# Splitting the second block's weights on POOL during the last feed-forward stage

## The chip, the cores and the metric

The kernel runs on one core of a Trainium2 chip. The time is device microseconds of one execution, taken as the median of 3 runs. TensorE (PE in the rows) multiplies, VectorE (DVE), ScalarE (ACT) and GpSimd (POOL) work on tiles in SBUF, and SyncE (SP) issues most of the DMAs.

## The reference, cut to what matters

The program is a model of two parts on 512 tokens of 1024 channels, batch 1, in float32. The first part has two layers, each with a mixer, cross attention and a gated feed-forward stage with a convolution over three tokens; the second part is one block that mixes a recurrence over chunks of 64 tokens with banded attention:

```
first_block, for layer in 0, 1:
    x = layer_norm(alpha * x + mixer(x))
    x = layer_norm(alpha * x + cross_attend(x, mem))
    x = layer_norm(alpha * x + conv_ffn(x))        # up: 1024 -> 2 x 2816, down: 2816 -> 1024
second_block:
    h = rms_norm(x, norm_g) * (1 + scale) + shift
    proj = h @ w_in                                # 1024 -> 2176 (r, k, v, g, decays) + 2048 (q, k, v, g)
    y_r = rwkv7_mix(token_shift(proj[:, :2176]))   # 8 heads of 64, a state per head
    y_a = chunk_band_attention(proj[:, 2176:])     # 8 heads of 64, 9 chunks of 64 keys
    x = x + gate * (concat(y_r * silu(g_r), y_a * silu(g_a)) @ w_out)
```

Weights are inputs, so each is read from HBM once per execution (two of the `w_in` slices twice).

## The kernel before

Activations lie with channels on the 128 partitions, 8 tiles of 128x512. A matmul in float32 is done as three products in float32r (`mm3`, lines 261 to 265): each operand is kept as a high part, rounded to float32r, and a low part, the remainder. So a weight piece of 128x1024 is loaded as it is into a `raw` tile (`piece`, line 239; SP issues the DMA), ScalarE casts it into the high half of a tile of the weight ring (line 229) and another engine subtracts to get the low half (line 230). In the first part that engine is VectorE; in the second block, where `self.extra` is 0, it is POOL. The ring has four `w` tiles, and two more (`wx`) while the first part runs; there are two `raw` tiles and a third (`rawx`) in the first part.

`lin` (line 267) does a product with stationary weights: for each block of 128 output channels, 24 matmuls (8 channel tiles, three products) into a PSUM bank, and then a function `epi` on the result. `ffn` (line 619) is the feed-forward stage. It goes through the 22 tiles of 128 inner channels in three chunks of 8, 8 and 6. For each inner tile there are two blocks upward; the gate's result goes through the convolution and a gelu, the other is multiplied with it and split into an `hd` tile (22 of these upward steps a layer). After each chunk 8 blocks go downward and are added to the residual `x` (lines 648 and 650). At the end of the last chunk POOL sums `x` and its squares over the channel tiles (`res_stat`, lines 370 and 371) for the layer norm (`ln_half`), and takes part in the norm itself (line 400).

`open2` (line 723) starts the second block while the last norm is going on: it computes the blocks `OPEN = (16, 0, 4, 8, 1)` of `w_in`. `block2` then has one line of work with long waits: four head pairs (`rwkv_pair`, line 866), the inversion of each chunk's triangular matrix (`rwkv_invert`, line 991, 31 steps of lines 1003 and 1005 on VectorE), and the chain of states (`rwkv_chain`). All else, the other blocks of `w_in`, attention and the start of `w_out`, stands as generators in `ORDER` (line 48): `r` and `q` are blocks of `w_in`, `v` the attention's values, `g` gates, `p` and `a` attention, `y` gated results and `o` the output. `fill` (line 775) puts some microseconds of it wherever the line of work waits; each entry may start only at its milestone (the number beside it). `lin_g` (line 839) is such a block; it gets its weights through `piece` too, as do `att_v` (line 1129), `out_begin` and `out_end`.

No queue's order is written out by hand as a whole. A planner orders each engine's instructions by the program's order and by when it expects their inputs and tiles to be ready, so an engine's queue is not always in the order of the code. A tile's next user waits until all users of its former content are done.

Of the kernel before, what the change touches and what calls it, by code (L numbers as in the profile page):

```python
# [172 lines left out]
class Prog:  # L173
# [69 lines left out]

    def raw(self):
        self.n += 1
        if self.extra and self.n0 % 3 == 2:
            self.n0 += 1
            return self.t("rawx", [P, 1024], F32, 1)
        self.n0 += 1
        return self.keep.tile([P, 1024], F32, tag="raw", name=f"raw_{self.n}", bufs=2)  # L250

    def wtile(self):
        """The weights' ring: some of its room is there only in the first block."""
        self.nw += 1
        if self.extra and self.nw % (4 + self.extra) >= 4:
            return self.t("wx", [P, 2, 1024], F32R, self.extra)
        self.n += 1
        return self.keep.tile([P, 2, 1024], F32R, tag="w", name=f"w_{self.n}", bufs=4)
# [8 lines left out]
    def lin(self, src, ms, xs, epi, n=S, first=0, last=0):  # L267
        """The first (last) few blocks go through one half of the tokens, then through the other, for the LN
        before (after) them; epi(m, psum, tokens) gets the last ones by halves."""
# [43 lines left out]
    def flush(self):  # L313
        """The LN that is due."""
        while self.pending:
            ts = self.pending.pop(0)
            self.ln_half(ts)
            if self.norm[0] == "ln_ffn_g" and self.norm[2] == 1:
                self.modulate(ts)

    def lin_tm(self, src, pieces, xs, ntok, epi):
        """out[tok tiles][128, 512 cols]: activations stationary, weights moving."""
        banks = [self.bank() for _ in range(ntok)]
        for j, pc in enumerate(pieces):
            w = self.piece(self.a[src][pc])
            for kk in range(2):
                k = 2 * j + kk
                cs = slice(kk * 512, kk * 512 + 512)
                for s in range(ntok):
                    ss = slice(s * P, s * P + P)  # L330
                    self.mm3(banks[s], (xs[k][0][:, ss], xs[k][1][:, ss]), (w[:, 0, cs], w[:, 1, cs]),
                             k == 0, k == 7)
        for s in range(ntok):
            epi(s, banks[s])
# [8 lines left out]
    def rsqrt(self, y, t, v, eps):  # L343
        """y = (v + eps) ** -0.5: the table's value and a Newton step; eps is a column of self.eps."""
# [7 lines left out]
    # residual, then LN over the channels  # L352
# [61 lines left out]
    # mixer of layer 0  # L414
# [204 lines left out]
    def ffn(self, l, xs):  # L619
        nc = self.nc  # L620
        for c, (f0, f1) in enumerate(CHUNKS):
# [3 lines left out]
            def epi(m, ps, ts):  # L625
# [9 lines left out]
                else:  # L635
                    h = self.tmp()
                    nc.vector.tensor_tensor(out=h, in0=ps, in1=keep["g"], op=ALU.mult)
                    hs.append(self.split(self.hd(), h))

# [5 lines left out]
            def epi_d(m, ps, ts):  # L645
# [5 lines left out]
                if c == 1 and l == 0 and m == 1:  # L651
                    self.ada_end()
                if c == 2:
                    self.res_stat(m, ts)
# [5 lines left out]
    # the modulation of the second block, gathered a piece at a time  # L660
# [23 lines left out]
    def ada_end(self):  # L684
        nc = self.nc
        # the sum over the partitions: within 32 of them by turning 32-blocks, then over the four groups
# [18 lines left out]
    def modulate(self, ts):  # L705
        """rms_norm(x) * norm_g * (1 + scale) + shift of half of the tokens."""
# [16 lines left out]
    def open2(self):  # L723
        """The second block's first products, of the first half of the tokens."""
# [48 lines left out]
    # The second block has one line of work with long waits (the states) and much other work for the tensor  # L773
    # engine: `bg` holds the latter as generators, and fill() puts some of it wherever the former waits.
# [57 lines left out]
    def mm(self, out, **kw):  # L832
        """A product on the line with the waits: it stays behind what fill() put before it."""
        self.tc.keep_in_program_order(self.nc.tensor.matmul(out, **kw))  # L834
# [4 lines left out]
    def lin_g(self, src, m, xs, epi, ks=range(KT)):  # L839
        w = self.piece(self.a[src][m])  # L840
# [25 lines left out]
    def rwkv_pair(self, j):  # L866
        """What the chunks of heads 2j and 2j+1 need."""
# [9 lines left out]
        # kk  # L877
# [12 lines left out]
        # k'  # L890
        nc.scalar.activation(u, av, AF.Identity, bias=self.ka1[:, j : j + 1], scale=self.v("k_a_2", j))
        nc.vector.tensor_tensor(out=k, in0=k, in1=u, op=ALU.mult)
        # bonus
# [7 lines left out]
        # decays  # L901
# [20 lines left out]
        # values by token  # L922
# [20 lines left out]
        # scores within the chunks  # L943
# [25 lines left out]
        # keys by token  # L969
# [10 lines left out]
        # the part of the right sides that no state enters  # L980
# [10 lines left out]
    def rwkv_invert(self, prs):  # L991
        """(I - N)^-1 of each chunk's strictly triangular N: 32-blocks by substitution, then the block between."""
# [58 lines left out]
    def rwkv_chain(self, prs, tt):  # L1051
# [40 lines left out]
        def line(i, pr):  # L1092
            for _ in chunks(i, pr):
                yield FILL[9]
            # group norm, then the gate
# [33 lines left out]
    def att_v(self, half, xs):  # L1129
        """Values of two token tiles."""  # L1130
        self.va += [self.t("va", [P, S], F32, 4) for _ in range(2)]
        banks = [self.bank() for _ in range(2)]
        for jj in range(4):
            w = self.piece(self.a["in_va"][jj])
# [12 lines left out]
    def att_epi(self, m, ps):  # L1147
        """Queries or keys of a pair of heads, normed."""
# [15 lines left out]
    def att_probs(self, j):  # L1164
        """Softmax of a pair of heads: a tile holds a chunk's queries of one head, then of the other."""
# [60 lines left out]
    def gate_epi(self, n):  # L1226
        """silu(x) = (tanh(x / 2) + 1) * x / 2; the half comes where it is used."""
# [22 lines left out]
    def out_begin(self):  # L1250
        """The residual, and the first products of w_out over what is there."""
# [5 lines left out]
        for m in range(NPART):  # L1257
            w, ps = self.piece(self.a["out"][m]), self.bank(("mm", "mm", "ch", "ch")[m])
# [9 lines left out]
    def out_end(self, out):  # L1268
        nc = self.nc
        rest = [k for k in range(KT) if k not in KS]  # L1270
        for m in range(8):
# [4 lines left out]
            else:  # L1276
                w, ps = self.piece(self.a["out"][m]), self.bank()
# [93 lines left out]
```

## Time and profile before

| | us |
|---|---|
| median of 3 runs | 1856.92 (1856.45 to 1857.71) |
| span of the profiled execution, first to last instruction | 1854.5 |
| PE busy | 1786.7 (96%) |
| VectorE busy | 1096.3 (59%) |
| ScalarE busy | 783.0 (42%) |
| POOL busy | 362.8 (20%) |

The median is 2.4 us above the span of the profiled execution. Stages in the trace: the last feed-forward stage runs from about 1046 to 1400 us, the norm and the opening to about 1437, pairs to about 1600, the inversion to 1661, the states to about 1800, the output to the end. A matmul's duration in a row is longer than the distance between two starts, since matmuls overlap. POOL's and VectorE's durations are from issue to end, so an instruction that stands still on its engine shows as a long one. A wait is put down to the releaser that came last.

### The profile page before, as it was taken

To read this page: it belongs to the slowest core of one execution; us is meant where nothing else is said; L and a number is where in the kernel's file an instruction comes from. 1 tells how busy PE (TensorE), PEld (TensorE's weight loads), DVE (VectorE), ACT (ScalarE), POOL (GpSimd) and SP (SyncE) were. 2 spreads that over 40 slices of the span, in tenths; PEclk is the share of its full clock that TensorE was granted. 3 is DMA by queue.
4 is the path that set the end of the run, shared out by engine and by line. 5 is a ranking of instruction groups with operands and counts; after the bars stand their busy time and mean duration, and the time that the engine had idled before them with its cause. 6 is when DMAs were issued, how large, how long until landed. Compare 5 with 4: busy or idle time off the path is not lost.

```text
span 1854.5 us, 26344 instructions
## 1 busy us (share of the span) xinstructions
PE 1786.7 (96%) x10476; PEld 1502.4 (81%) x10476; DVE 1096.3 (59%) x1741; ACT 783.0 (42%) x1319; POOL 362.8 (20%) x331
## 2 busy tenths in 40 slices
PE   8999998999999999999999999999998888879999
PEld 7889988888888888988998988888887766656657
DVE  5676689743463467444565764343447666975673
ACT  5444534532332356232453642232335645535561
POOL 0115014000000051000501400000015455623232
PEclk9999999999999999999999999999999999989999
DMA  8431455332322226333131242323222222222142
GB/s 279 145 103 60 132 181 188 100 102 91 102 92 91 80 64 196 112 96 100 59 104 35 69 125 92 102 92 100 88 86 73 82 75 88 89 74 81 56 160 103
DMA packets 62635, 192.25 MB, mean 104 GB/s; under 512 B 7344, under 2 KB 10032, under 8 KB 62512
## 3 DMA queue, kind: packets, MB, share of 16 engines
q1 hardware_dynamic: 54432, 172.25, 29.0%
q0 software_dynamic: 3248, 9.44, 1.5%
q10 hardware_dynamic: 4832, 8.88, 1.4%
q8 instruction: 82, 1.34, 0.3%
q14 instruction: 41, 0.34, 0.1%
HBM read 181.36 MB, written 9.18 MB: 103 GB/s over the span
## 4 chain that ended last, share of the span: by engine, by line
PE 76%; DVE 15%; ACT 3%; issue 3%; DMA 2%; POOL 0%; SPq 0%; DVEq 0%; ACTq 0%; POOLq 0%
PE ch L264 10%; PE ch L263 10%; PE ch L265 10%; PE mm L263 9%; PE mm L265 9%; PE mm L264 9%; PE pv L264 3%; PE pv L263 3%; PE pv L265 3%; PE ch L834 3%; DVE x L401 2%; DVE xh L405 1%; DVE w L230 1%; DVE x L400 1%; DVE vt L681 1%
## 5 line engine op out<-in xcount | busy, mean ns | idle before, releaser
L263 PE MATMUL mm<-xh,w 128*128 128x512 f32 (+1 forms) x704 | 266.1, 378 | 8.5 <-ACT w L229 7.5
L265 PE MATMUL mm<-xh,w 128*128 128x512 f32 (+1 forms) x704 | 258.6, 367 | 0.8 <-DVE w L230 0.8
L264 PE MATMUL mm<-xh,w 128*128 128x512 f32 (+1 forms) x704 | 259.0, 368 | 0.0
L370 POOL TENSOR_TENSOR t<-x,x 128x512 f32<-128x512 f32 x6 | 8.1, 1351 | 1011.1 <-ACT w L229 656.1
L229 ACT CAST w<-raw 128x1024 fp32r<-128x1024 f32 (+2 forms) x131 | 133.1, 1017 | 164.0 <-PE ch L265 62.9
L263 PEld LDWEIGHTS mm<-xh,w 128*128 128x128 f32 x704 | 135.6, 193 | 35.7 <-ACT w L229 7.8
L264 PE MATMUL ch<-xh,w 128*128 128x512 f32 (+1 forms) x432 | 154.1, 357 | 0.6 <-DVE xh L405 0.5
L264 PEld LDWEIGHTS mm<-xh,w 128*128 128x128 f32 x704 | 135.9, 193 | 22.9 <-issue 3.4
L263 PE MATMUL ch<-xh,w 128*128 128x512 f32 (+1 forms) x432 | 153.0, 354 | 1.3 <-ACT xh L404 1.3
L265 PE MATMUL ch<-xh,w 128*128 128x512 f32 (+1 forms) x432 | 152.7, 353 | 1.5 <-DVE w L230 1.5
L265 PEld LDWEIGHTS mm<-xh,w 128*128 128x128 f32 x704 | 135.8, 193 | 22.6 <-issue 1.1
L229 ACT CAST wx<-raw 128x1024 fp32r<-128x1024 f32 (+1 forms) x85 | 88.1, 1039 | 152.4 <-PE ch L265 71.5
L230 DVE TENSOR_TENSOR w<-rawx,w 128x1024 fp32r<-128x1024 f32 (+2 forms) x85 | 104.1, 1225 | 68.0 <-ACT w L229 67.6
L229 ACT CAST w<-rawx 128x1024 fp32r<-128x1024 f32 (+2 forms) x85 | 87.3, 1027 | 116.4 <-PE mm L265 71.0
L230 DVE TENSOR_TENSOR w<-raw,w 128x1024 fp32r<-128x1024 f32 (+2 forms) x90 | 113.0, 1257 | 37.8 <-ACT w L229 37.4
L230 DVE TENSOR_TENSOR wx<-raw,wx 128x1024 fp32r<-128x1024 f32 (+1 forms) x85 | 107.6, 1267 | 27.6 <-ACT wx L229 27.4
L230 POOL TENSOR_TENSOR w<-raw,w 128x1024 fp32r<-128x1024 f32 x41 | 100.4, 2456 | 119.0 <-ACT w L229 115.1
L263 PE MATMUL ch<-xh,wx 128*128 128x512 f32 (+1 forms) x304 | 103.5, 341 | 0.0
L265 PE MATMUL ch<-xh,wx 128*128 128x512 f32 (+1 forms) x304 | 103.0, 339 | 0.0
L264 PE MATMUL ch<-xh,wx 128*128 128x512 f32 (+1 forms) x304 | 103.0, 339 | 0.0
L263 PE MATMUL mm<-hd,w 128*128 128x256 f32 (+1 forms) x304 | 97.7, 322 | 3.6 <-ACT hd L229 3.6
L265 PE MATMUL mm<-hd,w 128*128 128x256 f32 (+1 forms) x304 | 97.9, 322 | 0.0
(484 smaller groups left out, 4498.6 us busy)
## 6 DMA issues: line engine op xcount, KB each, us to landing
raw<-in_up SPq DMA_DIRECT2D x56, 512.0 KB, 3.5
rawx<-in_up SPq DMA_DIRECT2D x32, 512.0 KB, 3.5
kt<-in_ada SPq DMA_DIRECT2D x48, 256.0 KB, 3.3
raw<-in_dn SPq DMA_DIRECT2D x24, 512.0 KB, 3.5
raw<-in_in_r SPq DMA_DIRECT2D x24, 512.0 KB, 3.5
raw<-in_c_in SPq DMA_DIRECT2D x16, 512.0 KB, 3.5
raw<-in_xo SPq DMA_DIRECT2D x12, 512.0 KB, 3.6
raw<-in_xv SPq DMA_DIRECT2D x11, 512.0 KB, 4.1
```

Of the source, the lines that this page charges most:

```text
L229: nc.scalar.copy(hi, src)
L230: (eng or nc.vector).tensor_tensor(out=lo, in0=src, in1=f32(hi), op=ALU.subtract)
L263: mm(out, lhsT=ah, rhs=bh, start=start, stop=False)
L264: mm(out, lhsT=ah, rhs=bl, start=False, stop=False)
L265: mm(out, lhsT=al, rhs=bh, start=False, stop=stop)
L370: eng.tensor_tensor(out=sz, in0=self.x[0][:, ts] if m == 1 else sz, in1=z, op=ALU.add)
L400: (nc.vector if k in DVE_SUB else nc.gpsimd).tensor_tensor(out=x, in0=x, in1=mn, op=ALU.subtract)
L401: nc.vector.scalar_tensor_tensor(out=x, in0=x, scalar=gk, in1=rs, op0=ALU.mult, op1=ALU.mult)
L405: nc.vector.scalar_tensor_tensor(out=lo, in0=x, scalar=bk, in1=f32(hi), op0=ALU.add, op1=ALU.subtract)
L681: nc.vector.scalar_tensor_tensor(out=dst, in0=raw, scalar=sc, in1=dst, op0=ALU.mult, op1=ALU.add)
L834: self.tc.keep_in_program_order(self.nc.tensor.matmul(out, **kw))
```

## The change

A preparation stage is added to the last feed-forward stage (`l == 1`). `pre_begin` lists the weight pieces of the second block in the order of their first use, without those of `OPEN`: 36 pieces, with the four of `in_va` once. `pre_step` is called after each of the 22 upward steps and after the 16 downward steps of the first two chunks. A call loads the next piece from POOL's queue into the lower half of a `vt` tile (two of 128x2x1024, which the attention before has left), after a copy of one column from the step's result into that place; that copy ties the load to the stage's progress. Then POOL does the split of the piece of the call before, copy and subtraction, and stores both halves, 1 MB, in HBM. In the second block `ready` takes the place of `piece` at all four callers: SP loads the finished 1 MB straight into a tile of the weight ring, with no cast on ScalarE and no subtraction on POOL there. The entry `(0, "r1")`, which computed block 1 once more though `OPEN` has it, leaves `ORDER`. The other lines of the diff take away comments.

```diff
@@ ORDER
-    (0, "r1"), (0, "r5"), (0, "r9"),
+    (0, "r5"), (0, "r9"),
@@ class Prog
+    def pre_begin(self):
+        self.prep, todo = {}, []
+        for _, ws in ORDER:
+            for w in ws.split("+"):
+                k, m = w[0], int(w[1:])
+                if k in "rq" and m not in OPEN:
+                    todo.append(("in_r", m))
+                elif k == "g":
+                    todo.append(("in_r", 12 + m) if m < 4 else ("in_ga", m - 4))
+                elif w == "v0":
+                    todo += [("in_va", i) for i in range(4)]
+                elif k == "o":
+                    todo += [("out", i) for i in range(8)]
+        self.todo, self.due2 = todo, []
+
+    def pre_step(self, at):
+        nc = self.nc
+        if self.todo:
+            key = self.todo.pop(0)
+            t = self.t("vt", [P, 2, D], F32, 2)
+            nc.gpsimd.tensor_copy(t[:, 1, 0:1], at[:, 0:1])
+            nc.gpsimd.dma_start(out=t[:, 1, :], in_=self.a[key[0]][key[1]])
+            self.due2.append((key, t))
+        if len(self.due2) > 1 or not self.todo:
+            for key, t in self.due2[:1]:
+                self.due2.pop(0)
+                hi, lo = t[:, 0, :].bitcast(F32R), t[:, 1, :].bitcast(F32R)
+                nc.gpsimd.tensor_copy(hi, t[:, 1, :])
+                nc.gpsimd.tensor_tensor(out=lo, in0=t[:, 1, :], in1=t[:, 0, :], op=ALU.subtract)
+                name = f"sp_{key[0]}{key[1]}"
+                d = self.prep[key] = self.dram.tile([P, 2, D], F32, tag=name, name=name)
+                nc.gpsimd.dma_start(out=d, in_=t)
+
+    def ready(self, src, m):
+        w = self.wtile()
+        self.nc.sync.dma_start(out=f32(w), in_=self.prep[src, m])
+        return w
@@ ffn
+        if l == 1:
+            self.pre_begin()
...
                     hs.append(self.split(self.hd(), h))
+                    if l == 1:
+                        self.pre_step(f32(hs[-1][:, 0, :]))
...
+                if c < 2 and l == 1:
+                    self.pre_step(x)
@@ lin_g
-        w = self.piece(self.a[src][m])
+        w = self.ready(src, m)
@@ att_v
-            w = self.piece(self.a["in_va"][jj])
+            w = self.ready("in_va", jj)
@@ out_begin
-            w, ps = self.piece(self.a["out"][m]), self.bank(("mm", "mm", "ch", "ch")[m])
+            w, ps = self.ready("out", m), self.bank(("mm", "mm", "ch", "ch")[m])
@@ out_end
-                w, ps = self.piece(self.a["out"][m]), self.bank()
+                w, ps = self.ready("out", m), self.bank()
```

## Rows read from the trace of the kernel before

**Rows 1.** Stretches, feed-forward: us, busy PE, PEld, DVE, ACT, POOL, clock, DMA share, GB/s

```profile
1140.00:1180.00 40.00, 40.00 (x173) 32.23 (x172) 13.89 (x15) 7.64 (x8) 0.00 (x0) 1.00 0.28 92
```

**Rows 2.** The same view, pair stage

```profile
1480.00:1520.00 40.00, 35.07 (x190) 25.80 (x188) 29.65 (x44) 17.08 (x24) 22.38 (x16) 0.87 0.24 70
```

**Rows 3.** Waits of PE from 1398 us: total us, times, longest us

```profile
PE ch L834 <- DVE rt L894: 17.8, 4, 4.9
PE at L710 <- ACT kt L408: 6.4, 3, 2.7
PE at L1157 <- ACT t L1153: 6.0, 2, 5.8
```

**Rows 4.** Timeline of DVE, pair 1: start us, us, instruction

```profile
1499.97 0.43 DVE L349 TENSOR_SCALAR rt<-rt 128x512 f32<-128x512 f32 x1
...
1508.31 2.96 DVE L894 SCALAR_TENSOR_TENSOR rt<-rk,vec,rk 128x512 f32<-128x512 f32 x1
```

**Rows 5.** Timeline of POOL, pair 1

```profile
1501.61 1.66 POOL L905 TENSOR_TENSOR rt<-rt,rt 128x512 f32<-128x512 f32 x1 [7.02 <-DVE rt L904]
1503.23 2.86 POOL L230 TENSOR_TENSOR w<-raw,w 128x1024 fp32r<-128x1024 f32 x1
1506.04 1.79 POOL L914 TENSOR_TENSOR ar<-rk,rt 128x512 f32<-128x512 f32 x1
```

**Rows 6.** Timeline of DVE, inversion; the second and last rows bound five long ones

```profile
1604.40 4.37 DVE L349 TENSOR_SCALAR t<-t 128x512 f32<-128x512 f32 x1
...
1610.95 2.33 DVE L1003 TENSOR_TENSOR rt<-c,c 128x87 f32<-128x87 f32 x1
...
1637.54 0.37 DVE L1003 TENSOR_TENSOR rt<-c,c 128x207 f32<-128x207 f32 x1
1637.95 2.56 DVE L1005 TENSOR_TENSOR c<-c,rt 128x207 f32<-128x207 f32 x1
```

**Rows 7.** Timeline of POOL, inversion

```profile
1637.92 2.36 POOL L230 TENSOR_TENSOR w<-raw,w 128x1024 fp32r<-128x1024 f32 x1 [10.02 <-ACT w L229]
```

**Rows 8.** Groups of POOL, whole span: count, busy us, mean ns, idle before

```profile
L230 POOL TENSOR_TENSOR w<-raw,w 128x1024 fp32r<-128x1024 f32 x41 | 100.4, 2456 | 119.0 <-ACT w L229 115.1 <-DMA raw<-in_in_r 3.5
...
L966 POOL DMA_DIRECT2D dn<-mk x16 | 9.3, 588 | 12.2 <-DVE mk L960 12.2
...
L452 POOL COPY t<-t 128x1 f32<-128x1 f32 x4 | 0.8, 202 | 8.4 <-ACT t L447 8.4
```

**Rows 9.** Stretches of half clock: columns of rows 1; one of six, their sum

```profile
1510.60:1517.50 6.90, 6.17 (x17) 4.13 (x18) 6.30 (x10) 0.72 (x1) 5.01 (x4) 0.51 0.17 14
...
sum 34.60, PE 27.82 PEld 18.12 DVE 29.84 ACT 6.54 POOL 21.65; mean PE 4.64 PEld 3.02 DVE 4.97 ACT 1.09 POOL 3.61
```

**Rows 10.** Groups of ACT, 1437 to 1855 us

```profile
L229 ACT CAST w<-raw 128x1024 fp32r<-128x1024 f32 x40 | 41.8, 1045 | 33.9 <-PE mm L265 19.0 <-DMA raw<-in_in_r 8.2 <-DMA raw<-in_out 6.6
```

**Rows 11.** Timeline of DVE, feed-forward: upward steps 1 and 8, downward 9 and 10

```profile
1072.80 0.69 DVE L230 TENSOR_TENSOR hd<-t,hd 128x512 fp32r<-128x512 f32 x1
...
1135.86 0.68 DVE L230 TENSOR_TENSOR hd<-t,hd 128x512 fp32r<-128x512 f32 x1
1139.23 0.69 DVE L648 SCALAR_TENSOR_TENSOR x<-x,pv 128x512 f32<-128x512 f32 x1 [2.68 <-PE pv L265]
...
1144.83 0.69 DVE L648 SCALAR_TENSOR_TENSOR x<-x,ch 128x512 f32<-128x512 f32 x1 [3.29 <-PE ch L265]
```

**Rows 12.** DMA issues: engine, count, KB each, median us to landing

```profile
raw<-in_in_r SPq DMA_DIRECT2D x24, 512.0 KB, 3.5
...
raw<-in_dn SPq DMA_DIRECT2D x10, 384.0 KB, 2.9
...
c<-dn POOLq DMA_DIRECT2D x1, 512.0 KB, 3.6
dt<-c POOLq DMA_DIRECT2D x1, 512.0 KB, 2.9
```

**Rows 13.** Timeline of POOL, end of the feed-forward stage

```profile
1384.79 1.29 POOL L370 TENSOR_TENSOR t<-x,x 128x512 f32<-128x512 f32 x1 [327.63 <-ACT w L229]
```

## The prediction

> **What bounds the kernel now.** I read the page's slices first, then the stretch table (busy time of each engine in chosen windows), then who TensorE waited for, then the single instructions around those waits. The last feed-forward stage (1046 to about 1400 us) has TensorE busy in every microsecond, VectorE at a third and POOL at nothing [rows 1]. The second block (from 1437 us) is different: TensorE is busy 35.1 of 40 us in the pair stage, at a granted clock of 0.87 [rows 2]. Of its waits 17.8 us are four waits of a pair's TensorE work for VectorE's line 894, 6.0 us end at line 1157 in the inversion, and 6.4 us lie in the norm before the block [rows 3].
>
> Why VectorE is late there is seen in single instructions. In pair 1 a scaling of a 128x512 tile takes 0.43 us, but line 894, a product of the same size, 2.96 us [rows 4], while POOL runs without a pause: line 905, then a weight subtraction of 2.86 us, then line 914 [rows 5]. In the inversion line 1003 needs 0.37 us and line 1005 of the same shape, just behind it, 2.56 us; the long one ends just behind POOL's subtraction of 2.36 us [rows 6, 7]. So a VectorE instruction that reads two SBUF tensors, or copies or scales within SBUF, stands still while POOL reads SBUF. Here 41 weight subtractions, mean 2.4 us, do that to a line of work that TensorE waits for [rows 8].
>
> **The change part by part.**
>
> *Subtractions leave the second block.* In each pair the subtraction stands between POOL's lines 905 and 914 and takes about 2.86 us out of the chain to line 894 [rows 5]; four pairs give 11.4 us. The four waits are 17.8 us in all, the longest 4.9 [rows 3], so about 1.6 us of each stays: POOL's own 905, 914, 915 and 919 (twice) go on blocking. Bounds 6 to 17.8, I take 11.4. In the inversion five of the 62 instructions of lines 1003 and 1005 are about 2.1 us longer than their neighbours, and one scaling takes 4.37 us [rows 6], where the same scaling takes 0.43 us unblocked [rows 4]: 10.5 + 3.9 = 14.4 us leave that chain. TensorE idles at line 1157 for 6.0 us of that stretch, so no more than this comes back: 6.0 (0 to 6.0). In the norm one subtraction falls into the last of three waits (6.4 in all): 1.5 (0 to 2.1).
>
> *Clock.* Around these waits the granted clock falls to its lower level, 1.2 GHz: six stretches, 34.6 us, granted 0.51, with TensorE busy for 27.8 of them, cost 0.49 x 27.8 = 13.6 us [rows 9]. With the waits cut to a third some of these falls should stay away; I take half, 7 (0 to 13.6).
>
> *Casts leave ACT.* 40 of 1.05 us [rows 10]. They are mostly beside other work; one stands in the chain of pair 0: 1 (0 to 3).
>
> *`r1` goes.* Block 1 is computed in the opening too; 24 matmuls, as many as lie between two downward results 5.60 us apart [rows 11], are 5.6 us of TensorE time. But `r1` is fill for pair 0, and the fill allowed there runs out (only `r5`, `r9` remain), so the chain decides and most of the 5.6 becomes idle time: 1.5 (0 to 5.6).
>
> *Loads of finished weights.* 40 loads of 1 MB replace 41 of 512 KB on SP. From 384 KB at 2.9 and 512 KB at 3.5 us [rows 12], 0.6 us per 128 KB, 1 MB lands in 5.9 us. The queue behind a load is the next load; each waits for a weight tile of four, so it is issued three blocks (over 16 us) ahead, which hides 5.9. The cover is gone at the end: `o0` to `o3` hold all four tiles. There a tile that comes free is refilled by a cast and a subtraction, 1.05 + 2.4 = 3.5 us [rows 8, 10], beside three short products; 5.9 is 2.4 us more. I take 2 lost (0 to 4).
>
> *36 preparations move into the feed-forward stage*, one per step: 20 upward steps and 16 downward ones. One is a copy of one column (0.2), a load issued from POOL (0.6, landing 3.6 after issue), a full-width copy, a subtraction (2.4), a store of 1 MB (0.6 to issue) [rows 8, 12]. The full copy isn't in the trace: at least 0.2 (a one-column copy), at most 2.4 (two inputs of that size); I take 1.3, the middle, since it has one input of that subtraction's two. POOL was idle, so only two things can reach TensorE. First, VectorE: 3.7 us of blocking an item, where it is busy 13.9 of 40 us [rows 1]. Its weight splits run five blocks ahead (six tiles); the last split of a chunk ends at 1136.5 and the first result that depends on it is out at 1139.2 [rows 11], so a block of 2.4 us there can cost up to 2.4, three times: 2 lost (0 to 7). Second, lateness, which is decided by the period p of one item when POOL is behind: 0.2 + 3.6 + 1.3 + 2.4 + 0.6 = 8.1 us. The first step is at 1072.8, the first downward one (the ninth) at 1139.9 [rows 11], and POOL's first due work in this stage is at 1384.79 [rows 13]. If POOL is behind from the first step on, the last item ends at 1073 + 36 x 8.1 = 1365, if from the ninth on, at 1140 + 28 x 8.1 = 1367: 18 us early, cost nothing. The limit is p = 8.7. With the copy at 2.4, p = 9.2 and the end is 1404, 19 us late.
>
> The Trainium skill, GPSIMD Engine Reference, Engine selection, says that an operation with one input runs on GpSimd at about line rate; its section on elementwise cycle accounting gives 1.03 cycles an element for light loops. By that the copy is an estimated 0.9 us and the end is 14 us earlier still, with the same sum. No row shows it.
>
> This is for the queue order load, copy, subtract, store. That POOL's queue isn't the program's order is seen where a background subtraction stands between lines 905 and 914, which are neighbours in the code without any fill between them [rows 5].
>
> Sum: 11.4 + 6 + 1.5 + 7 + 1 + 1.5 - 2 - 2 = 24.4 us off the profiled 1854.5 us span. The median of the runs is 1856.92, 2.4 us above, which is outside the span and stays: 1832.5.
>
> **Rivals.**
>
> *A, POOL comes late (slower).* If the queue keeps the code's order, the one-column copy of item n+1 waits for the store of item n-1, issued just ahead of it, since there are two `vt` tiles; that waiting copy holds up the subtraction and everything else on POOL. A store of 512 KB lands in 2.9 us [rows 12]; with 0.6 per 128 KB 1 MB is 5.3. Then p = 5.3 + 0.2 + 0.6 + 1.3 + 2.4 = 9.8, the last item ends at 1073 + 353 = 1426, 41 us after POOL is due. The sums of the norm, paced by the last products, catch up some 3, so 38 us of TensorE idle less the 24 won: 1870. It is slower from p = 9.4 on, where 36 x (p - 8.7) passes the gain. For it: the two tiles, and 1.5 MB an item beside DMA traffic of 92 GB/s [rows 1]. Against it: the reordering seen. The Trainium skill, DMA: Bandwidth & Descriptors, anatomy of one DMA, says that the receipt of a write takes most of the fixed 2 us and longest where the target is HBM, which speaks for A. The rows disagree: the 512 KB store to HBM lands in 2.9 us, the load in 3.6 [rows 12]. By the page's formula a 1 MB store is an estimated 4.4 us and p = 8.9, 7 us late, 1839.
>
> *B, the waits are refilled.* POOL's five own operations in a pair (1.7 and 1.8 us the two shown, some 8 in all) block VectorE next and the half clock stays: half of 11.4, 3 of the inversion, none of the rest, less 4: about 5 us, 1852. For it: line 894 started at 1508.31, when the subtraction had been over for 2.2 us [rows 4, 5]. Against it: POOL is a queue; what starts 2.86 earlier ends earlier.
>
> *C, the change doesn't hide what it says.* The blocking moves to the feed-forward stage and costs TensorE its full 7 us there, and the 1 MB loads 0.2 us each of 40: 24 - 5 - 8 = 11 us, 1846.
>
> **How the numbers follow.** Likeliest 0.62 (own range 1812 to 1848), A 0.20, B 0.12, C 0.06. The forecast is the likeliest case's 1832.5. The best corner is all listed waits, clock and `r1`, near 1800; the range goes from 1808 to 1866, leaving out the upper half of A and that corner. This kernel can tell 0.2% (3.7 us) from no change. Faster: 0.61 + 0.04 of A + 0.06 of B + 0.05 of C = 0.76; same: 0.03 of A, 0.05 of B, 0.01 of C = 0.09; slower: 0.13 of A and 0.02 of the others = 0.15.
>
> **What would show it.** Right: POOL busy some 4 us a step from 1073 to 1370 with its first sum still near 1385; TensorE full until 1400; lines 1003, 1005 and 349 in the second block without instances over 2 us; line 894's wait near 6 us in all; fewer half-clock windows between 1480 and 1660. Wrong: POOL's line 370 starting late in that stage with TensorE waiting behind the norm (A); the waits unchanged though the subtractions are gone (B). A copy over 2 us, or stores that the next item waits for, makes the forecast wrong.

## The result, and the profile after

The changed kernel is slower: 1884.31 us against 1856.68 us, a ratio of 1.0153 (95% interval 1.0129 to 1.0177). The prediction was 1832.5 us, faster. Its profiled execution took 1889.03 us with a span of 1887.2 us, 32.7 us more than the span of before. In the changed kernel's rows line numbers from the preparation on are higher by 41 to 47: lines 349, 370, 710, 894, 1003, 1005 and 1027 of before are 390, 411, 757, 941, 1050, 1052 and 1074.

Who TensorE waited for, from 1380 us to the end of the changed kernel (total us, times, longest us), as in [rows 3]:

```profile
PE at L429 <- POOL t L411: 55.0, 2, 54.8
PE ch L881 <- DVE rt L941: 10.1, 4, 2.9
PE ch L881 <- DVE rt L1074: 6.6, 1, 6.6
PE at L757 <- ACT kt L449: 5.3, 2, 2.7
PE mm L304 <- DMA w<-sp_out: 2.0, 1, 2.0
```

One wait of 54.8 us is new and larger than the whole loss; a long time like this in which TensorE has nothing to do is called a stand below. Line 411 is POOL's first sum of the last norm. It started at 1384.79 in [rows 13]; here it starts at 1441.64, right behind the last preparation's store:

```profile
1438.42 2.33 POOL L274 TENSOR_TENSOR vt<-vt 128x1024 fp32r<-128x1024 f32 x1
1441.05 0.57 POOL L277 DMA_DIRECT2D sp_out<-vt  x1 [0.30 <-POOL vt L274]
1441.64 1.27 POOL L411 TENSOR_TENSOR t<-x,x 128x512 f32<-128x512 f32 x1
```

So POOL came late (rival A of the prediction), and by more than A had it. Why is seen in POOL's timeline of one item of an upward step (an item is the preparation of one weight piece; in brackets stands the idle time ahead of an instruction, and who ended it):

```profile
1282.36 0.57 POOL L277 DMA_DIRECT2D sp_in_r<-vt  x1 [0.30 <-POOL vt L274]
1282.93 0.26 POOL L266 COPY vt<-hd 128x1 f32<-128x1 f32 x1
1283.49 0.54 POOL L267 DMA_DIRECT2D vt<-in_in_r  x1 [0.30 <-POOL vt L266]
1290.38 1.04 POOL L273 CAST vt<-vt 128x1024 fp32r<-128x1024 f32 x1 [6.35 <-DMA vt<-in_in_r]
1291.50 2.39 POOL L274 TENSOR_TENSOR vt<-vt 128x1024 fp32r<-128x1024 f32 x1
1294.19 0.57 POOL L277 DMA_DIRECT2D sp_in_r<-vt  x1 [0.30 <-POOL vt L274]
```

From one store's issue to the next, at 1282.36 and 1294.19, are 11.8 us. More than half of it POOL stands and waits for the load that it has just issued. The load is issued 1.1 us behind a 1 MB store and takes 6.9 us from its issue to the cast. Eleven items run like this one, in two stretches at 13.2 and 12.6 us from store to store (1097 to 1163 and 1258 to 1334 us). Seventeen go two by two, both loads ahead of both subtractions, at 9.4 us an item from 1173 to 1258 and 8.2 from 1344 to 1410; there POOL waits for stores more than for loads. POOL's waits from 1060 to 1442 us put these together; the 30-odd pauses of 0.3 us stand between a POOL instruction and the DMA that follows it:

```profile
POOL vt L273 <- DMA vt<-in_in_r: 71.4, 15, 8.2
POOL vt L273 <- DMA vt<-in_in_va: 27.3, 4, 8.3
POOL vt L266 <- DMA sp_in_r<-vt: 27.1, 10, 6.1
POOL vt L273 <- DMA vt<-in_out: 19.6, 5, 5.4
...
POOL vt L267 <- POOL vt L266: 9.8, 33, 0.3
```

Waits for loads are 126 us (with 7.8 of the gate pieces), waits for stores 42 us. The first subtraction ends at 1078.6 and the last at 1440.75: 35 periods of 10.35 us, where the prediction had 8.1 and a limit of 8.7.

The feed-forward stage itself did not get longer for TensorE. The stretch that answers to [rows 1], in its columns, and behind it the second block from its first normed products to one and the same product of its last output block, some 3 us before the last:

```profile
1140.00:1180.00 40.00, 40.00 (x174) 32.27 (x173) 16.37 (x14) 7.38 (x7) 16.12 (x15) 1.00 0.65 226
...
1464.90:1880.30 415.40, 393.01 (x2715) 288.91 (x2716) 262.86 (x632) 182.44 (x382) 69.99 (x86) 0.96 0.41 147
```

Before, the second block's stretch lasted from 1409.3 to 1847.7, 438.4 us. It starts 55.6 us later and is 23.0 us shorter: together the 32.6 us of the result. The long instances of lines 1003 and 1005 in the inversion [rows 6] are gone; no instance of line 1050 is over 0.43 us (minimum, median and maximum in ns), and line 1052's longest is 426 ns too:

```profile
L1050 DVE TENSOR_TENSOR rt<-c,c x31: 193/358/426, 1646.4 to 1673.3; 128x31 f32<-128x31 f32 x2, 128x60 f32<-128x60 f32 x2, 128x87 f32<-128x87 f32 x2, 128x112 f32<-128x112 f32 x2
```

### The profile page after: what moved, and what is told of

The parts are those of the page before. It is cut to its first block, busy times and chain, and to the rows that moved or that the text cites. A ratio compares the mean times of both kernels' runs of the same rounds, so it can differ in the third digit from the quotient of the medians.

```text
span 1887.2 us, 26434 instructions
## 1 busy us (share of the span) xinstructions
PE 1780.0 (94%) x10452; PEld 1498.7 (79%) x10452; DVE 1100.3 (58%) x1739; ACT 743.2 (39%) x1277; POOL 444.3 (24%) x470
## 4 chain that ended last, share of the span: by engine, by line
PE 76%; DVE 12%; DMA 5%; ACT 3%; issue 3%; POOL 1%; SPq 0%; DVEq 0%; ACTq 0%; POOLq 0%
PE ch L305 10%; PE ch L304 10%; PE ch L306 10%; PE mm L304 9%; PE mm L305 9%; PE mm L306 9%; PE pv L305 3%; PE pv L304 3%; PE pv L306 3%; PE ch L881 3%; DMA vt<-in_out 2%; DVE x L442 1%; DVE xh L446 1%; DVE w L230 1%; DVE x L441 1%
## 5 line engine op out<-in xcount | busy, mean ns | idle before, releaser
L304 PE MATMUL mm<-xh,w 128*128 128x512 f32 (+1 forms) x696 | 260.6, 374 | 6.3 <-ACT w L229 6.1
L306 PE MATMUL mm<-xh,w 128*128 128x512 f32 (+1 forms) x696 | 254.0, 365 | 0.8 <-DVE w L230 0.8
L305 PE MATMUL mm<-xh,w 128*128 128x512 f32 (+1 forms) x696 | 254.5, 366 | 0.0
L304 PEld LDWEIGHTS mm<-xh,w 128*128 128x128 f32 x696 | 132.8, 191 | 32.8 <-ACT w L229 6.3
L305 PEld LDWEIGHTS mm<-xh,w 128*128 128x128 f32 x696 | 132.9, 191 | 22.9 <-issue 3.5
L306 PEld LDWEIGHTS mm<-xh,w 128*128 128x128 f32 x696 | 132.9, 191 | 21.6 <-DVE w L230 1.0
L230 DVE TENSOR_TENSOR w<-rawx,w 128x1024 fp32r<-128x1024 f32 (+2 forms) x85 | 109.2, 1285 | 66.6 <-ACT w L229 66.2
L230 DVE TENSOR_TENSOR w<-raw,w 128x1024 fp32r<-128x1024 f32 (+2 forms) x90 | 127.0, 1412 | 36.1 <-ACT w L229 35.6
L229 ACT CAST w<-raw 128x1024 fp32r<-128x1024 f32 (+2 forms) x90 | 90.3, 1004 | 128.8 <-PE ch L306 62.6
L230 DVE TENSOR_TENSOR wx<-raw,wx 128x1024 fp32r<-128x1024 f32 (+1 forms) x85 | 121.3, 1429 | 28.2 <-ACT wx L229 27.9
L229 ACT CAST w<-rawx 128x1024 fp32r<-128x1024 f32 (+2 forms) x85 | 87.3, 1027 | 114.4 <-PE mm L306 69.7
L304 PE MATMUL mm<-hd,w 128*128 128x256 f32 (+1 forms) x304 | 98.3, 324 | 3.6 <-ACT hd L229 3.6
L306 PE MATMUL mm<-hd,w 128*128 128x256 f32 (+1 forms) x304 | 98.4, 324 | 0.0
L305 PE MATMUL mm<-hd,w 128*128 128x256 f32 (+1 forms) x304 | 97.9, 322 | 0.0
```

The source lines that it names most:

```text
L229: nc.scalar.copy(hi, src)
L230: (eng or nc.vector).tensor_tensor(out=lo, in0=src, in1=f32(hi), op=ALU.subtract)
L304: mm(out, lhsT=ah, rhs=bh, start=start, stop=False)
L305: mm(out, lhsT=ah, rhs=bl, start=False, stop=False)
L306: mm(out, lhsT=al, rhs=bh, start=False, stop=stop)
```

## The experiments

**28 items.** The eight pieces of `out`, the last in the list, are not prepared, and a piece that isn't takes the old way.

```diff
-                elif k == "o":
-                    todo += [("out", i) for i in range(8)]
@@ ready
+        if (src, m) not in self.prep:
+            return self.piece(self.a[src][m])
```

> The eight pieces of `out` are left out of the preparation and go the old way in the tail (cast on ACT, subtraction on POOL): 28 items in place of 36. Theory L (all of the loss is one stand of TensorE of 54.8 us for POOL's first sum of the norm, queued behind the last eight items; the second block itself is 23 us shorter): in the changed kernel the 28th store was issued at 1374, before POOL's sums are due, so the stand goes, TensorE waits under 3 us at the norm and the time is 1884 - 54 + 2 = 1832 (1826 to 1840). Rival G (much of the 23 us was a gift of the stand: weights loaded and queues emptied while TensorE stood): the stand goes, but the block loses 10 us or more of its gain, 1842 or above. Rival D (the period of POOL's items is set by the traffic, so that they end late anyhow): the sums start after 1400.

1825.58 us against 1854.51 us for the kernel before beside it: 0.9849 (0.9831 to 0.9868), faster than both kernels. POOL has 10 us of room ahead of the sums, and TensorE's wait there is 0.2 us:

```profile
PE at L429 <- POOL t L411: 0.2, 1, 0.2
```

```profile
1372.30 0.57 POOL L275 DMA_DIRECT2D sp_in_ga<-vt  x1 [0.30 <-POOL vt L272]
1383.23 2.06 POOL L411 TENSOR_TENSOR t<-x,x 128x512 f32<-128x512 f32 x1 [10.35 <-ACT w L229]
```

The gain did not need the stand, so rival G falls. Theory L's time was 6 us too high, 0.4 us outside its range: the time fell by 59 us, 4 more than the stand, and the second block took 408.3 us instead of 415.4.

**Two items.** Only two pieces are prepared, and all loads of finished weights read those two.

```diff
-        self.todo, self.due2 = todo, []
+        self.todo, self.due2 = todo[:2], []
@@ ready
-        self.nc.sync.dma_start(out=f32(w), in_=self.prep[src, m])
+        self.nc.sync.dma_start(out=f32(w), in_=list(self.prep.values())[m % 2])
```

> Only two pieces are prepared; all loads of the second block read one of these two from HBM, so the block's weights are wrong and its traffic and instructions are the changed kernel's. This is the gain without the preparation. Theory L: no stand and nothing on POOL in the feed-forward stage, 1832 (1826 to 1838), and equal to the run with 28 items within 4 us if the preparation costs TensorE nothing before 1395. Rival G: 1842 or above. Rival V (the preparation slows VectorE and so TensorE in the feed-forward stage): faster than the run with 28 items by 4 us or more.

1824.2 us, 0.9845 (0.9826 to 0.9864): the same as with 28 items. So no cost of the preparation to TensorE is seen as long as POOL is done in time, though VectorE is held up by it: over 335 us of the feed-forward stage VectorE is busy 152.1 us with two items and 187.7 us with 28, TensorE 335.0 and 334.4. (The two runs also differ in the eight pieces of `out`, which are finished here and not there, so equal times alone don't prove it. The norm's first products start at 1404.9 us here and at 1407.7 with 28; in the two kernels without any preparation, before and without `r1`, they start at 1409.3 and 1406.4. A cost under some 3 us can't be seen.)

```profile
1060.00:1395.00 335.00, 335.00 (x1580) 280.02 (x1580) 152.14 (x175) 109.02 (x139) 22.20 (x22) 1.00 0.33 104
```

```profile
1060.00:1395.00 335.00, 334.38 (x1575) 279.26 (x1576) 187.71 (x179) 111.03 (x144) 156.87 (x152) 1.00 0.66 226
```

**The cost alone.** All items are prepared, none is used.

```diff
@@ ready
-        w = self.wtile()
-        self.nc.sync.dma_start(out=f32(w), in_=self.prep[src, m])
-        return w
+        return self.piece(self.a[src][m])
```

> All 36 items are prepared and stored, but the second block loads and splits its weights the old way. Theory L: the stand of about 55 us stays and the gain goes, except for the 5.6 us of products that the dropped `r1` saved: 1884 + 17 = 1901 (1895 to 1910). Rival G: the old block too would profit from the stand, by 5 us or more: below 1895.

1914.1 us, 1.0325 (1.0305 to 1.0346), 13 us above the expectation and 4 above its range. The stand is 55.9 us, and the old waits are back: four of 18.4 us for VectorE in the pairs, 5.6 us in the inversion, 6.0 us in the norm. Rival G falls here too; the finished weights are worth about 30 us to the changed kernel (1914.1 less 1884.3, from runs beside different runs of before). The kernel without `r1` (below) and this stand come to 1848.5 + 55.9 = 1904; what the other 10 us are was not settled.

**Stores from SP.**

```diff
-                nc.gpsimd.dma_start(out=d, in_=t)
+                nc.sync.dma_start(out=d, in_=t)
```

> The stores of the 36 items are issued from SP's queue, not from POOL's. The load of an item then no longer lies in one queue behind the store of the item before. Theory Q (the load takes 6.8 us and not 3.6 because it queues behind the 1 MB store, and POOL stands for it): loads land in about 3.6 us, an item takes 0.2 + 0.9 + 3.6 + 1.1 + 2.4 = 8.2 us, the last one ends near 1370, no stand, 1832 (1826 to 1842). Rival D (the DMA engines' traffic, not the queue, sets 6.8): loads still land in over 5.5 us, an item takes over 10 us, the stand stays over 30 us and the time over 1860. Rival S (the stores hold up the weight loads behind them on SP): TensorE waits in the feed-forward stage for weights, some us in all.

1973.48 us, 1.0648 (1.0632 to 1.0664). Theory Q's expectation fell: POOL still waits 6.8 us for a load. Rival D's loads and period came, but not its stand (0.2 us); rival S decided the time. SP's queue and POOL's, one item:

```profile
1144.08 0.33 SPq L277 DMA_DIRECT2D sp_in_va<-vt  x1
1144.50 0.38 SPq L241 DMA_DIRECT2D rawx<-in_dn  x1
1144.99 0.84 SPq L241 DMA_DIRECT2D raw<-in_dn  x1
1156.64 0.33 SPq L277 DMA_DIRECT2D sp_in_va<-vt  x1
```

```profile
1145.48 0.57 POOL L267 DMA_DIRECT2D vt<-in_in_va  x1 [0.30 <-POOL vt L266]
1152.86 1.29 POOL L273 CAST vt<-vt 128x1024 fp32r<-128x1024 f32 x1 [6.81 <-DMA vt<-in_in_va]
```

Every store on SP waits for POOL's subtraction of its item, and two weight loads wait behind it and start with it. So POOL's pace of 12.56 us an item becomes SP's, two blocks of weights in 12.56 us where TensorE uses one in 5.6, and TensorE stands in the feed-forward stage for splits of weights and of `hd` (rival S, over 100 us in all, against the "some us" expected). The item's load now flies beside a store and two more loads, so this run can't tell a shared queue from shared transfers; it does show that another queue alone doesn't help.

**POOL in the order of the code.** Each POOL instruction of the preparation is pinned behind the one ahead of it in the code.

```diff
+            pin = self.tc.keep_in_program_order
-            nc.gpsimd.tensor_copy(t[:, 1, 0:1], at[:, 0:1])
+            pin(nc.gpsimd.tensor_copy(t[:, 1, 0:1], at[:, 0:1]))
...
```

> POOL's instructions of the preparation are held in the order of the code: column copy and load of item n+1, then cast, subtraction and store of item n. In the changed kernel each load is followed at once by its own cast, and POOL stands for it. Theory O (that order is what makes an item take 10.3 us): the load flies beside the cast and subtraction of the item before; the next column copy waits for a store instead, 5.1 us, so an item takes 5.1 + 0.2 + 0.9 + 1.1 + 2.4 = 9.7 us at most, the last one ends by 1420, the stand is at most 35 us and the time 1864 or less. Rival D (traffic sets the period whatever the order): still over 10 us an item and 1880 or more.

1874.83 us, 1.0109 (1.0096 to 1.0123). That is 11 us over theory O's bound and 5 us under rival D's:

```profile
1261.43 0.18 POOL L267 COPY vt<-hd 128x1 f32<-128x1 f32 x1 [4.69 <-DMA sp_in_r<-vt]
1261.91 0.53 POOL L268 DMA_DIRECT2D vt<-in_in_r  x1 [0.30 <-POOL vt L267]
1262.43 1.05 POOL L275 CAST vt<-vt 128x1024 fp32r<-128x1024 f32 x1
1263.57 2.40 POOL L276 TENSOR_TENSOR vt<-vt 128x1024 fp32r<-128x1024 f32 x1
1266.28 0.58 POOL L279 DMA_DIRECT2D sp_in_r<-vt  x1 [0.30 <-POOL vt L276]
1271.52 0.18 POOL L267 COPY vt<-hd 128x1 f32<-128x1 f32 x1 [4.67 <-DMA sp_in_r<-vt]
```

The wait for the load is gone and a wait for the store has taken its place: 10.09 us an item in these rows, 10.2 on average. The expectation had left out the hand-over of 0.3 us ahead of the store. The stand is 44.9 us, 10 more than expected:

```profile
PE at L431 <- POOL t L413: 45.1, 2, 44.9
```

This is the order that rival A of the prediction assumed, and its 9.8 us. The order is thus not the cause by itself: with two tiles and one engine that waits in order, POOL stands for a transfer either way.

**No stores.** As in the run with two items, but all 36 are loaded, cast and subtracted.

```diff
-                nc.gpsimd.dma_start(out=d, in_=t)
+                if len(self.prep) <= 2:
+                    nc.gpsimd.dma_start(out=d, in_=t)
```

> All 36 items are loaded, cast and subtracted, but only the first two are stored, and the second block reads these two for all its weights (its output is wrong, its loads are as large as before). Theory W (the 1 MB stores are what makes loads land after 6.8 us and holds the tiles): loads land in 3.6 us, an item takes some 8.2 us where POOL is behind, the last one ends near 1370, no stand, 1826 (1822 to 1834). Rival O alone (POOL's order): loads that wait for nothing still make over 9.5 us an item, the stand stays over 20 us.

1844.04 us, 0.9943 (0.9925 to 0.9961), between the two expectations. The median load of an `in_r` piece lands 4.5 us after its issue, not 6.6; the last item and the first sum:

```profile
1390.94 1.04 POOL L273 CAST vt<-vt 128x1024 fp32r<-128x1024 f32 x1 [4.08 <-DMA vt<-in_out]
1392.06 2.38 POOL L274 TENSOR_TENSOR vt<-vt 128x1024 fp32r<-128x1024 f32 x1
1394.41 1.26 POOL L412 TENSOR_TENSOR t<-x,x 128x512 f32<-128x512 f32 x1
```

From the end of the first subtraction, 1079.07, to that of the last are 35 periods of 9.01 us. Even without stores POOL is over the limit of 8.7, and TensorE stands 7.9 us. So the stores are part of the lateness, and not all of it.

**`r1` alone.** The kernel before without the entry `(0, "r1")`, nothing else.

> The kernel before with nothing but the entry of `r1` in the second block's order taken out: its 24 products are computed in the opening anyhow. The prediction gave 1.5 us for it (0 to 5.6), since the waits of pair 0 would take up the rest. If the products were fill that nothing needed, 0 to 2 us faster; if TensorE was the limit there, 5.6 us faster, and then the gain of the finished weights is that much less.

1848.46 us, 0.9968 (0.9957 to 0.998): 5.7 us, as much as its products take.

**Sums on VectorE.** All 36 items; sums and subtractions of the last norm leave POOL.

```diff
-            eng = nc.vector if ts.start and m in DVE_ADD else nc.gpsimd
+            eng = nc.vector if self.norm[2] == 1 and self.norm[0] == "ln_ffn_g" else nc.gpsimd
...
```

> The changed kernel with all 36 items, but the sums and the subtractions of the last norm run on VectorE instead of POOL, so that nothing of the norm is queued behind the preparation. Theory L: the stand of 54.8 us goes though POOL still ends its items near 1440; VectorE has 12 sums and 10 subtractions more, up to 5 us: 1830 (1825 to 1838). Rival B (POOL's casts and subtractions stop VectorE in the norm, where TensorE waits for it): 1838 to 1850.

1837.11 us, 0.9903 (0.9886 to 0.9919): inside theory L's range by 0.9 us only, so what rival B names is not excluded. POOL's last item ends even later, at 1449.4, and the stand is gone: what made it was the norm's place behind the items on POOL. It is 11.5 us slower than with 28 items; the norm ends about 6 us later (TensorE's last wait in its first half, 5.4 us, ends at 1414.0 against 1407.7). The rest lies in the second block: it takes 416.3 us against 408.3, with TensorE busy 392.4 us for the same products at a mean granted clock of 0.96, against 384.6 at 0.98.

**32 items.** Half of the pieces of `out` are prepared. (Lines 429 and 411 are 431 and 413 here.)

> 32 items: the first four pieces of `out` are prepared too, the last four go the old way. Theory L (the loss is POOL's lateness, item by item): in the changed kernel the 32nd store was issued at 1406.3, 23 us after POOL's first sum is due (1383.2 in the run with 28 items); the sums take 9 us, TensorE has no work from 1395.5, so it stands until 1415, 20 us, and the time is 1825.6 + 20 = 1846 (1840 to 1852). Rival X (the loss comes with the last items alone, for another reason than the queue): within 4 us of 1825.6 or of 1884.

1848.39 us, 0.9962 (0.9947 to 0.9978), and the stand is the 20 us worked out before:

```profile
PE at L431 <- POOL t L413: 20.6, 2, 20.4
```

With 28, 32 and 36 items it is 0.2, 20.4 and 54.8 us.

**12 items.** Only `r` pieces and the values are prepared; those of queries, keys, gates and `out` go the old way. (Lines 941, 1204 and 1074 of the changed kernel are 939, 1202 and 1072 here; 1204 is 1157 of before.)

> Only the first 12 items are prepared: the pieces that the four pairs of the second block need first (`r` and the values). Those of the queries, keys and gates are split the old way beside pair 3, the inversion and the chain. Theory S (each subtraction costs where it stands in a waiting chain): the waits of pairs 0 to 2 stay at 2 to 3 us, TensorE's wait of 5.4 us in the inversion comes back, with it some half-clock time: 1834 (1829 to 1838). Rival E (each finished piece is worth the same, 22.9 us over 28 items): 16 x 0.82 = 13 us lost, 1839. Rival P (the pairs alone count): 1826 to 1829.

1838.41 us, 0.9913 (0.9889 to 0.9937). Rival P falls; the time lies 0.4 us over S's range and near E's 1839, and does not tell these two apart. TensorE's waits show more:

```profile
PE ch L879 <- DVE rt L939: 12.5, 4, 4.9
PE at L1202 <- ACT t L1198: 5.4, 1, 5.4
...
PE ch L879 <- DVE rt L1072: 3.3, 1, 3.3
```

The inversion's wait is back at exactly the 5.4 us of the kernel without `r1`, as S said. One of the four pair waits is back at 4.9 us too, and it is that of pair 2 (it ends at 1542.70 us), where S had pairs 0 to 2 unchanged.

The waits grow by 4.9 us against the run with 28 items (the one behind the inversion falls from 6.2 to 3.3 us), of 12.8 us lost; from 1405 to 1815 us the granted clock is 0.95, where 28 items have 0.98 in their second block. So the waits come back mostly where S said, and the time that this takes was put too low.

**Products held back.** With 28 items, POOL's two products of the decays wait for line 941.

```diff
         nc.vector.scalar_tensor_tensor(out=u, in0=r, scalar=self.v("r_k_2", j), in1=k, op0=ALU.mult, op1=ALU.mult)
+        bk = self.c5()[:, :1024].rearrange("p (c b t) -> p c b t", c=8, b=2)
+        nc.gpsimd.tensor_copy(bk[:, 0, 1, 0:1], u[:, 0:1])
...
-            nc.gpsimd.tensor_tensor(out=bk[hs, :, 1 - hh, :], in0=ch(k)[hs], in1=ch(c)[hs], op=ALU.mult)
+            pin(nc.gpsimd.tensor_tensor(out=bk[hs, :, 1 - hh, :], in0=ch(k)[hs], in1=ch(c)[hs], op=ALU.mult))
```

> The kernel with 28 items, and in each pair of the second block POOL's two products of the decays are held back behind VectorE's bonus product (line 941) by a one-column copy that reads it; the rest of POOL's pair work stays. In the changed kernel line 941 takes 2.96 to 2.99 us in all four pairs, beside POOL's products, though no weight subtraction is near. Theory B (VectorE's product of two SBUF tensors stands still while POOL reads SBUF; what is left of these waits is POOL's own pair work): line 941 falls to about 0.7 us, TensorE's four waits from 10.1 to 2 us or less, unless POOL's products are late for the next step: 1818 (1814 to 1823). Rival N (the product takes 3 us for a reason of its own): line 941 stays near 3 us and the time at 1825 or above. Rival T (the waits move to POOL's later products): line 941 falls, the time stays within 3 us of 1825.6.

1823.58 us, 0.9817 (0.9801 to 0.9833). Line 941 in the run with 28 items, and in this one (ns: minimum, median, maximum of four):

```profile
L941 DVE SCALAR_TENSOR_TENSOR rt<-rk,vec,rk x4: 2964/2979/2987, 1467.8 to 1561.9; 128x512 f32<-128x512 f32 x4
```

```profile
L941 DVE SCALAR_TENSOR_TENSOR rt<-rk,vec,rk x4: 735/738/743, 1473.4 to 1564.0; 128x512 f32<-128x512 f32 x4
```

TensorE's waits in this one:

```profile
PE at L881 <- POOL c L968: 4.4, 3, 2.2
...
PE ch L881 <- DVE rt L941: 1.6, 3, 0.9
```

With these two products out of its way line 941 is four times as fast, 2.98 to 0.74 us, as theory B has it, and rival N falls. But POOL still reads SBUF beside it: its product of line 964 (962 of the changed kernel) starts 0.16 us behind line 941 in all four pairs, and now POOL's is the slow one, with 1.71 us against 1.26 with 28 items:

```profile
1500.50 0.74 DVE L941 SCALAR_TENSOR_TENSOR rt<-rk,vec,rk 128x512 f32<-128x512 f32 x1
```

```profile
1500.66 1.71 POOL L964 TENSOR_TENSOR rt<-rt,rt 128x512 f32<-128x512 f32 x1 [1.31 <-DVE ar L962]
```

In the run with 28 items POOL had started the first of the two products 0.35 to 0.38 us ahead of line 941, and line 941 ended only when that product and the one behind it were over. So in these rows the engine that comes second is the one that waits, and the prediction's "stands still while POOL reads SBUF" is one half of it. The Trainium skill, SBUF — State Buffer, Who interferes with whom, says that a VectorE instruction with two SBUF inputs contends with a GpSimd instruction that reads SBUF, and the loser waits; these rows agree.

The time does what rival T said: TensorE's waits for line 941 go from 10.1 to 1.6 us, but 4.4 us of new ones end at the products that were held back, and other small ones add up. The medians are 2 us apart and the two intervals just touch (0.9833 and 0.9831), so a small gain over the 28 items is neither shown nor excluded.

## Why the prediction was wrong

**The step that failed** is "lateness, which is decided by the period p of one item when POOL is behind: 0.2 + 3.6 + 1.3 + 2.4 + 0.6 = 8.1 us", with its "18 us early, cost nothing". The parts of the sum, load, cast, subtraction, store, stand in this order in the items that run like the one shown above, as POOL's queue shows; these take 12 to 13 us. The full copy was even cheaper than assumed, mean 1.18 us for 1.3. The Trainium skill, GPSIMD Engine Reference, Elementwise — side-by-side cycle accounting, gave an estimated 0.9 us for it; the shortest casts here take 1.03. Three things were too small or missing. The load was priced at the 3.6 us of a load of before that has no such store ahead of it [rows 12]; behind a 1 MB store it takes 6.9 us, and with no store in flight still 4.4 to 4.5 us (already the first item's, issued at 1070.3 and cast at 1074.8). With 4.5 alone the sum is 9.0, over the limit. Then, five steps on one queue are not just their durations: the hand-overs of 0.3 us from a POOL instruction to the DMA behind it, twice an item, and the load's place behind the store's issue stood nowhere. And the waits for stores, which rival A has, are at nothing in this sum. On average over the 36 items POOL waits 3.5 us for loads (behind 0.5 for issuing one) and 1.2 us for stores, and spends 0.5 us on hand-overs and 0.4 us on the one-column copy, which was priced at 0.2. The prediction checked the sum's margin, 8.7 against 8.1, with one end raised, the copy; the load, the largest term, had no upper end at all. Raised by the 2.9 us that [rows 12] give for half a store it would have crossed the limit.

**Rival A** had the right mechanism, POOL's late sum with TensorE behind the norm, and the sign that it named came true. Its period of 9.8 us belongs to the order of the code; that order, run on the chip, takes 10.09 us an item and 1874.8 us, near its 1870. "Against it: the reordering seen" was the weak point: reordering does not make a queue faster. The order that the planner chose left POOL waiting mostly for its loads (126 us) and less for its stores (42 us), 10.35 us an item and 1884.3.

**The gain** was right in its mechanism, and its sum, 24.4 us without lateness, was 4.5 us small: with 28 items the kernel is 28.9 us faster (the eight pieces of `out` are left out of that run). Term by term, by the waits of the kernel without `r1` against the run with 28 items where the change alone has to be seen. Waits of TensorE without `r1`, and with 28 items behind line 1027 (now 1074):

```profile
PE ch L834 <- DVE rt L894: 18.3, 4, 5.3
...
PE at L1157 <- ACT t L1153: 5.4, 1, 5.4
PE ch L834 <- DVE rt L1027: 3.1, 1, 3.1
```

```profile
PE ch L881 <- DVE rt L1074: 6.2, 1, 6.2
```

The second block without `r1`, and with 28 items:

```profile
1406.40:1838.00 431.60, 394.46 (x2713) 288.54 (x2714) 300.95 (x632) 220.16 (x422) 169.50 (x126) 0.95 0.29 92
```

```profile
1407.70:1816.00 408.30, 384.59 (x2715) 283.04 (x2716) 268.96 (x632) 189.74 (x390) 89.30 (x94) 0.98 0.40 139
```

- *Pairs, 11.4 forecast*: 18.3 to 10.1 us, 8.2. Each wait stays at 2 to 3 us, not 1.6, since line 941 remains blocked by POOL's own products in all four pairs; it only starts earlier. That is the core of rival B, and the last experiment shows it, though B's time of 1852 was far off.
- *Inversion, 6.0*: the wait of 5.4 us goes, but the wait behind it, for line 1027 (1074 after), grows from 3.1 to 6.2 us. Net 2.3. What is late next was not asked there.
- *Norm, 1.5*: 1.1 (6.5 to 5.4 us).
- *Clock, 7*: about 10, an estimate. With the same products in the block from its first normed product on, TensorE is busy 394.5 us without finished weights and 384.6 with 28 items, at mean granted clocks of 0.95 and 0.98. In the changed kernel it is 393.0 us at 0.96: there most of this gain is missing.
- *Casts leave ACT, 1*: no wait of TensorE for a weight's cast is in the list of the kernel without `r1`, so nothing is seen of it.
- *`r1`, 1.5*: 5.7 us, the upper bound. The prediction let the pair's chain eat the products; all of their time came back.
- *1 MB loads at the tail, 2 lost*: one wait of 2.0 us for `w<-sp_out`, as forecast.
- *VectorE in the feed-forward stage, 2 lost*: nothing that can be measured; 28 items and two items give the same time. TensorE's only new wait in it in the changed kernel is 1.4 us.

Pairs, inversion, norm, clock and `r1` come to about 27 of the 28.9 us. That the forecast sum is near this is in part luck: the pairs and the inversion were put 7 us too high, the clock and `r1` 7 us too low.

**Rival C** fell with that last term.

What stays open: whether the slower load beside a store is a matter of the queue or of the transfers. Also open is what decides how often the clock falls in the second block (below), in the version with the sums on VectorE too. A third `vt` tile, the plain remedy for both orders, was not tried.

## What to carry to other kernels

When work is moved to an idle engine, that engine's next due instruction is the limit: give every term of an item's period an upper end, the transfers first, and price a transfer beside those that the change puts next to it, not as it flew without them. Work that is tied to progress and whose period is over the limit did not catch up here, so leave out the items that are needed last: without 8 of 36 the same change is 1.5% faster instead of 1.5% slower. With two tiles an engine that works in order waited for a load or for a store in both orders that were run, and the order chose which.

## What the runs showed of the hardware

The granted clock of the second block differs between kernels with the same products there. In its first four stretches of 60 us the mean (1.00 is the full clock, the lower level is half of it) is 0.95, 0.91, 0.94 and 0.91 in the changed kernel, and 1.00, 0.94, 0.97 and 0.94 with 28 items. The run without stores shows the changed kernel's four figures; its stand is 7.9 us, and it is 18 us slower than the one with 28 items. With 32 items a stand of 20.4 us costs 22.8 us, little more than itself. So a stand can cost more than its length, but these runs don't settle when.

Of VectorE and POOL, when both read two SBUF tensors, the one that came second waited: the same VectorE product took 2.98 us when POOL had started 0.4 us ahead and 0.74 us when it was itself 0.16 us ahead; then POOL's product took 1.71 us and not 1.26.

A store on the queue that feeds TensorE's weights cost far more than expected: 119 us over the kernel before, since SP then waits at every store for the slow engine.
